# Gate stage: both tiles of a pair turned by VectorE, and the sum of h and the gated embedding made by accumulating transfers

## The chip, the core and the metric

The kernel runs on one core of one Trainium2 chip. The metric is the device time of one execution in microseconds (us). One core has TensorE (in the profile PE for its matmuls, PEld for its weight loads), VectorE (DVE), ScalarE (ACT), GpSimd (POOL) and SyncE (SP); SP, POOL and ACT also issue transfers (DMAs), each in its own queue.

## What is computed

One layer of a streaming encoder on 2048 prompt frames and 32 sample frames of width 1024, in float32:

```python
hn = rmsnorm(h, g_mix)
proj = hn @ w_in                                  # 1024 x 3072
hA, bA, cA, zA, vB, zB = split(proj)              # each 512 wide
yA, new_conv = short_conv_mixer(hA, bA, cA, zA, ...)
yB, new_pool = pooling_mixer(vB, zB, ...)
h = h + concat([yA, yB]) @ w_out
gate = sigmoid(rmsnorm(h, g_ple) @ w_ple_gate)
h = h + (p @ w_ple) * gate
y = rmsnorm(h, g_final)
```

The change touches the last three lines alone: the gate's product of h with `w_ple_gate` (1024 x 1024), the sum `h + e * gate` with the embedding `e = p @ w_ple`, and the closing norm.

## The kernel before

The frames lie in 17 tiles: 16 of 128 frames and one of 32. Three stages follow one another: the input projection with the two mixers, the output projection (which also writes h to device memory as `h_d`, the embedding as `e_d`, and each frame's norm factor to `rs_h`), and the gate stage, in which the change lies. The gate stage takes the 32-frame tile first (`plain`), then seven pairs of 128-frame tiles in a loop, `g0` to `g12` in steps of two, then a last pair with code of its own (`last_pair`, `g14`).

**A pair's products.** A pair is multiplied with the gate weights by a scheme of seven products (Winograd's form of Strassen's multiplication), `seven`, L210. The weights' quarters and their differences (`W["11"]` to `W["T4"]`) stay in SBUF. Every float32 operand is split into a high part (a cast by ACT, L77) and a low part (a subtraction by VectorE, L78), and a product is 12 matmuls of 128x512 (L167): four chunks of the depth, three combinations of high and low part each. The products of a pair run in the order 11, 12, S2, S1, S3, S4, 22, into three banks X, Y and Z. `carry` (ACT copy, L1309) sets aside what a bank holds before it goes on accumulating. `out` ends a quarter of the result: VectorE adds what was set aside (L1317), ACT applies the sigmoid (L1318, or L1315 where nothing was set aside), VectorE multiplies the embedding with it in place (`ee`, L1320) and adds that to h in place (`hh`, L1321). `at` is (tile, half): the outputs come as (0,0), (1,1), (0,1), (1,0).

**A pair's frames.** For the products the tiles of h must stand turned, channels on partitions. `prep_g(i)` gives two steps, called between the products of the pair before (`{2: first, 3: second}`). In `first`, `turned_here(i + 1)` loads the second tile in four transfers of 32 partitions each (L1298), so laid out that one VectorE instruction (`nc.vector.transpose`, which turns every 32x32 block, L1300) leaves it turned in four column groups; `whole` is the view of these groups. In `second`, `turned(i)` loads the first tile in one transfer (L327), ACT copies its halves in another order of channels (`ho`, L1287), and TensorE turns them in eight 128x128 transposes into a PSUM bank (`pth`, L1289). VectorE makes the sums S1 to S4 (L1433), and `put` splits each of the seven operands.

**The end of a tile.** `done_g`, L1325: ACT squares h and sums it (L88), POOL makes the norm factor (L69, L73), VectorE scales h in place by it and the final gain (L1328), and POOL's queue stores it (L1329).

**What sets the order.** The code is written tile by tile, and a planner orders the instructions of each engine by dependences and its own estimates; an engine then takes them strictly in that order, waiting on semaphores. Buffers come from rings: `xh` has 3 buffers for the tiles of h in natural order, `ya` 5 for those of e and for h before and after the turn, `st` 4 for what is set aside and the gate, `cmb` 8 for split operands, PSUM has 6 banks for products and 2 for transposes. A load into a ring waits until the buffer's last reader is done.

Of the kernel before, what the change touches and what calls it, by code (L numbers as in the profile page):

```python
# [12 lines left out]
ALU = mybir.AluOpType  # L13
PSUM = bass.MemoryType.PSUM

P = 128
# [18 lines left out]
def trunk(ctx, tc, x_p, x_s, c_conv, c_pool, p_p, p_s, g_mix, w_in, conv_w, conv_b, pool_w,  # L35
          pool_scale, w_out, g_ple, w_gate, w_ple, g_fin, y_p, y_s, sc_p, sp_p, sc_s, sp_s):
    nc = tc.nc
# [17 lines left out]
    def tbank(name):  # L55
        return ps_t.tile([P, 512], F32, tag="tr", name=name)
# [19 lines left out]
    def split(hi, lo, src, eng=nc.vector):  # L76
        ins = nc.scalar.copy(hi, src)  # L77
        eng.tensor_tensor(lo, src, hi.bitcast(F32), op=ALU.subtract)  # L78
        return ins
# [227 lines left out]
    def ring4(t, name):  # L307
        return t.tile([P, D], F32, tag="t", name=name)
# [15 lines left out]
    def load_rows(pool, name, i, pr, sa=None):  # L324
        r, n = tiles[i]
        t = ring4(pool, f"{name}_{i}")
        nc.sync.dma_start(t[:n], pr[r:r + n] if sa is None else rows_of(pr, sa, r, n))  # L327
        return t

    with ExitStack() as s1:  # L330
# [263 lines left out]
        for c, x in enumerate([*ahead0, short0]):  # L594
            normal(x)
            n = P if c < 3 else DEC
# [511 lines left out]
    with ExitStack() as s2:  # L1108
# [13 lines left out]
        def half_of(x, at, n=P):  # L1122
            return x[at[0]][:n, at[1] * NH:at[1] * NH + NH]
# [96 lines left out]
        for i in range(0, NT - 1, 2):  # L1220
# [6 lines left out]
            if last:  # L1227
                n = tiles[NT - 1][1]
# [50 lines left out]
        def turned(i):  # L1279

            r, n = tiles[i]
            t = load_rows(ya, "hn", i, h_d).rearrange("p (q k c) -> p k q c", q=4, k=KC)
            out = []
            for half in range(2):
                pt = tbank(f"pth_{i}_{half}")
                o = qa.tile([P, KH, P], F32, tag="q", name=f"ho_{i}_{half}")
                nc.scalar.copy(o[:n].rearrange("p k (q c) -> p k q c", q=4), t[:n, half * KH:half * KH + KH])  # L1287
                for k in range(KH):
                    nc.tensor.transpose(pt[:, k * P:k * P + n], o[:n, k], ident[:n, :n])  # L1289
                out.append(pt.rearrange("p (k t) -> p k t", k=KH))  # L1290
            return out

        def turned_here(i):

            r, n = tiles[i]
            t = ring4(ya, f"hn_{i}")
            for q in range(4):
                nc.sync.dma_start(t[q * 32:q * 32 + 32].rearrange("p (g c) -> p g c", g=4),  # L1298
                                  h_d[r:r + P, q * 256:q * 256 + 256].rearrange("(g p) c -> p g c", p=32))
            nc.vector.transpose(t, t)  # L1300
            u = t.rearrange("p (g k t) -> p k g t", g=4, k=KC)
            return u[:, :KH], u[:, KH:]

        def gate_ops(h, e, n, name, i):
            scale = lambda at: rs_h[:n, i + at[0]:i + at[0] + 1]

            def carry(ps, at):
                t = st.tile([P, NH], F32, tag="t", name=f"c_{name}_{at[0]}{at[1]}")
                nc.scalar.copy(t[:n], ps[:n])  # L1309
                return t  # L1310

            def out(ps, c, at):
                if c is None:
                    c = st.tile([P, NH], F32, tag="t", name=f"g_{name}_{at[0]}{at[1]}")
                    nc.scalar.activation(c[:n], ps[:n], AF.Sigmoid, scale=scale(at))  # L1315
                else:
                    nc.vector.tensor_tensor(c[:n], ps[:n], c[:n], op=ALU.add)  # L1317
                    nc.scalar.activation(c[:n], c[:n], AF.Sigmoid, scale=scale(at))  # L1318
                ee, hh = half_of(e, at, n), half_of(h, at, n)
                nc.vector.tensor_tensor(ee, ee, c[:n], op=ALU.mult)  # L1320
                nc.vector.tensor_tensor(hh, hh, ee, op=ALU.add)  # L1321

            return carry, out

# [97 lines left out]
        def prep_g(i):  # L1422

            A = {}
            whole = lambda t: t.rearrange("p k (g t) -> p k g t", g=4)

            def put(q, src, view=lambda t: t):
                A[q] = cmb.tile([P, KH, 2, P], F32R, tag="c", name=f"g{i}_{q}")
                split(view(A[q][:, :, 0]), view(A[q][:, :, 1]), src)

            def comb(q, x, y, op, view=lambda t: t):
                t = ss.tile([P, KH, P], F32, tag="s", name=f"g{i}_f{q}")
                nc.vector.tensor_tensor(view(t), x, y, op=op)  # L1433
                return t

            lower = []

            def first():
                lower.extend(turned_here(i + 1))

            def second():
                a21, a22 = lower
                s1 = comb("S1", a21, a22, ALU.add, whole)
                a11, a12 = turned(i)
                put("11", a11)
                s2 = comb("S2", s1, a11, ALU.subtract)
                s3 = comb("S3", whole(a11), a21, ALU.subtract, whole)
                put("12", a12)
                put("S2", s2)
                s4 = comb("S4", a12, s2, ALU.subtract)  # L1450
                put("S1", s1)
                put("S3", s3)
                put("S4", s4)
                put("22", a22, whole)

            S[i] = A
            return {2: first, 3: second}

        S = {}
        n = tiles[NT - 1][1]  # L1460
        A = short("gl", turned(NT - 1), n)
        for step in prep_g(0).values():
            step()
# [5 lines left out]
        for i in range(0, NT - 3, 2):  # L1469
            A = S.pop(i)  # L1470
            h = [load_rows(xh, "h", i + b, h_d) for b in range(2)]
            e = [load_rows(ya, "e", i + b, e_d) for b in range(2)]
            seven(f"g{i}", A, W, *gate_ops(h, e, P, f"g{i}", i), prep_g(i + 2))
            for b in range(2):
                done_g(i + b, h[b])
# [30 lines left out]
```

## Time and profile before

| | |
|---|---|
| median of 3 runs | 947.03 us (945.0 to 947.33) |
| the profiled execution, its span | 947.7 us |
| instructions in it | 13126 |
| mean granted TensorE clock | 0.989 of full speed |
| gate stage, first product of the first pair to the end | 777.6 to 947.7 us of the span |

The span runs from the first to the last instruction of the profiled execution, which is one execution by itself and not one of the three runs; no time outside its span is recorded. The profile lists for each instruction its engine, its line in the kernel, the tiles it writes and reads, its start and duration, and what ended the idle time before it. The stage tables give busy time by engine in a stretch, with the number of instructions in brackets, then the granted TensorE clock (PEclk), the share of the DMA engines that was busy, and GB/s. Rows of transfers give the size and the median time from issue to landing.

### The profile page before, as it was taken

The page shows a single profiled execution, that of the slowest core. Times are in us where ns is not written, and L with a number is a line of the kernel's source. Part 1 is how long each engine was busy: PE and PEld are TensorE (multiplying, and loading weights), DVE is VectorE, ACT ScalarE, POOL GpSimd, SP SyncE. Part 2 cuts the span into 40 slices and gives each one's busy share as a digit, 9 for nine tenths or more (in the row PEclk, how much of TensorE's full clock was granted, in tenths as well). Part 3 has the DMA queues.
Part 4 walks back from the last instruction along what each step waited for, and adds up shares of the span by engine and source line. Part 5 has one row for each costly group of instructions (what it writes and reads, how often), then busy time and mean ns, then how long its engine had stood idle before and what let it go on. Part 6 is the DMA issues. An engine that isn't in the chain of part 4 may idle for free.

```text
span 947.7 us, 13126 instructions
## 1 busy us (share of the span) xinstructions
PE 925.3 (98%) x4599; PEld 835.1 (88%) x4599; DVE 716.6 (76%) x1212; ACT 480.9 (51%) x890; POOL 136.3 (14%) x262
## 2 busy tenths in 40 slices
PE   6999999898999999999999999999999999999996
PEld 5999999898999999999999987888877868888885
DVE  6697999798677876776777588766554798888995
ACT  5554555463444454443454355434424875556564
POOL 2112323230100110000000011111111000211113
PEclk8999999899999999999999999999999999999999
DMA  8346586676973554628655349874785883566552
GB/s 243 102 127 193 170 273 201 224 219 192 406 273 93 166 183 135 219 56 285 178 175 175 130 146 291 288 200 146 228 253 161 304 285 123 197 232 226 208 206 111
DMA packets 132639, 190.05 MB, mean 201 GB/s; under 512 B 11740, under 2 KB 101084, under 8 KB 131293
## 3 DMA queue, kind: packets, MB, share of 16 engines
q1 hardware_dynamic: 115149, 134.06, 45.1%
q0 software_dynamic: 14688, 49.65, 15.9%
q10 hardware_dynamic: 2736, 5.51, 1.7%
q8 instruction: 36, 0.59, 0.2%
q14 instruction: 30, 0.25, 0.1%
HBM read 129.59 MB, written 59.58 MB: 200 GB/s over the span
## 4 chain that ended last, share of the span: by engine, by line
PE 74%; DMA 5%; DVE 2%; issue 2%; ACT 1%; POOL 1%; POOLq 0%; DVEq 0%; ACTq 0%; SPq 0%
PE x_g L167 9%; PE x_o L167 8%; PE x_zab L571 6%; PE z_g L167 5%; PE x_zbv L571 4%; PE e L102 4%; PE x_ch L571 4%; PE z_o L167 4%; PE z_zab L571 3%; PE z_ch L571 2%; PE y_g L167 2%; PE z_zbv L571 2%; PE y_o L167 2%; PE b L571 2%; PE zb L571 2%; PE h L571 2%
## 5 line engine op out<-in xcount | busy, mean ns | idle before, releaser
L77 ACT CAST y_S<-y_fS 128x512 fp32r<-128x512 f32 x32 | 19.5, 621 | 43.0 <-PE x_o L167 20.2
L571 PE MATMUL x_zab<-B,w_zab_S 128*128 128x416 f32 x168 | 36.6, 367 | 3.1 <-ACT V L866 2.8
L102 PE MATMUL e<-wq,pps 128*128 128x512 f32 (+1 forms) x156 | 38.9, 399 | 0.2 <-ACT pps L77 0.2
L406 DVE SCALAR_TENSOR_TENSOR xt<-xt,rstd_x,g_bc 128x1024 f32<-128x1024 f32 (+2 forms) x18 | 23.1, 1282 | 20.1 <-POOL rstd_x L73 18.7
L571 PE MATMUL z_ch<-B,w_ch_S 128*128 128x416 f32 x168 | 35.3, 360 | 2.4 <-ACT U L866 2.4
L571 PEld LDWEIGHTS x_zab<-B,w_zab_S 128*128 128x128 f32 x168 | 32.7, 197 | 4.4 <-ACT V L866 3.2
L167 PE MATMUL x_g<-wg_b,g_S 128*128 128x512 f32 x128 | 35.9, 390 | 0.0
L167 PE MATMUL x_o<-wo_b,y_S 128*128 128x512 f32 x128 | 35.8, 391 | 0.0
L571 PEld LDWEIGHTS z_ch<-B,w_ch_S 128*128 128x128 f32 x168 | 32.0, 192 | 3.2 <-ACT U L866 2.8
L571 PE MATMUL z_zab<-B,w_zab_S 128*128 128x416 f32 x168 | 34.7, 356 | 0.0
L571 PE MATMUL z_zbv<-B,w_zbv_S 128*128 128x416 f32 x168 | 34.2, 352 | 0.0
L571 PE MATMUL x_zbv<-B,w_zbv_S 128*128 128x416 f32 x168 | 34.1, 351 | 0.0
L571 PE MATMUL x_ch<-B,w_ch_S 128*128 128x416 f32 x168 | 34.0, 351 | 0.0
L102 PEld LDWEIGHTS e<-wq,pps 128*128 128x128 f32 (+1 forms) x156 | 27.4, 182 | 6.9 <-ACT pps L77 0.5
L571 PEld LDWEIGHTS z_zab<-B,w_zab_S 128*128 128x128 f32 x168 | 32.2, 192 | 0.4
L69 POOL TENSOR_SCALAR ms_f<-ssq_f 128x1 f32<-128x1 f32 (+1 forms) x15 | 8.8, 588 | 160.7 <-ACT junk L88 160.7
L571 PEld LDWEIGHTS x_ch<-B,w_ch_S 128*128 128x128 f32 x168 | 31.4, 188 | 0.3
L571 PEld LDWEIGHTS x_zbv<-B,w_zbv_S 128*128 128x128 f32 x168 | 31.3, 188 | 0.3
L571 PEld LDWEIGHTS z_zbv<-B,w_zbv_S 128*128 128x128 f32 x168 | 31.3, 188 | 0.4
L77 ACT CAST y<-y 128x512 fp32r<-128x512 f32 x24 | 14.8, 618 | 30.8 <-PE x_o L167 14.0
L1328 DVE SCALAR_TENSOR_TENSOR h<-h,rstd_f,g_bc 128x1024 f32<-128x1024 f32 (+1 forms) x15 | 19.3, 1284 | 12.7 <-POOL rstd_f L73 12.7
L167 PEld LDWEIGHTS x_o<-wo_b,y_S 128*128 128x128 f32 x128 | 23.9, 188 | 5.1 <-ACT c_o L1132 0.3
(582 smaller groups left out, 2670.3 us busy)
## 6 DMA issues: line engine op xcount, KB each, us to landing
y<-y_d SPq DMA_DIRECT2D x16, 512.0 KB, 6.4
x<-in_x_prompt_dram SPq DMA_DIRECT2D x16, 512.0 KB, 6.5
h_d<-x SPq DMA_DIRECT2D x16, 512.0 KB, 3.4
h<-h_d SPq DMA_DIRECT2D x16, 512.0 KB, 4.6
xt<-in_x_prompt_dram SPq DMA_DIRECT2D x15, 512.0 KB, 12.3
e<-e_d SPq DMA_DIRECT2D x15, 512.0 KB, 5.9
out_dram<-h POOLq DMA_DIRECT2D x14, 512.0 KB, 3.0
p_dT<-T POOLq DMA_DIRECT2D x12, 512.0 KB, 5.0
```

Source lines behind the costliest of these rows:

```text
L69: nc.gpsimd.tensor_scalar(ms[:n], ssq[:n], scalar1=1.0 / D, scalar2=EPS, op0=ALU.mult, op1=ALU.add)
L77: ins = nc.scalar.copy(hi, src)
L102: nc.tensor.matmul(ps[:n], pps[:, a, k, :n], wp[k][b][:, cs], start=k + q == 0, stop=k == 1 and q == 2)
L167: nc.tensor.matmul(ps[:n], lhs[:, k, a, :n], w[b][:, k], start=start and k + q == 0, stop=k == KH - 1 and q == 2, skip_group_check=True)
L406: nc.vector.scalar_tensor_tensor(xt[:n], xt[:n], r[:n], g_bc[:n], op0=ALU.mult, op1=ALU.mult)
L571: nc.tensor.matmul(ps[:, :NB], lhs[:, k, x], b[:, k, y], start=start and k + q == 0, stop=stop and k == KH - 1 and q == 2, skip_group_chec ...
L1328: nc.vector.scalar_tensor_tensor(h[:n], h[:n], rf[:n], g_bc[:n], op0=ALU.mult, op1=ALU.mult)
```

## The change

Two edits, both in the gate stage.

In `gate_ops`, for full tiles, the addition of the gated embedding `ee` to `hh` by VectorE becomes a transfer from `ee` to `hh` (SBUF to SBUF, 128 x 512, 256 KB) that adds to what it finds there; it is issued by POOL. There are four a pair, for the seven pairs of the loop. The 32-frame tile and the last pair keep VectorE's addition.

In `prep_g`, both tiles of a pair are loaded and turned by `turned_here`, in the step `first`. `turned` is used for the 32-frame tile alone. The operands made from the first tile are read from SBUF in the view `whole`, where they were read from PSUM.

```diff
                 ee, hh = half_of(e, at, n), half_of(h, at, n)
                 nc.vector.tensor_tensor(ee, ee, c[:n], op=ALU.mult)
-                nc.vector.tensor_tensor(hh, hh, ee, op=ALU.add)
+                if n == P:
+                    nc.gpsimd.dma_start(hh, ee, accum_op=ALU.add)
+                else:
+                    nc.vector.tensor_tensor(hh, hh, ee, op=ALU.add)
...
-            lower = []
+            both = []

             def first():
-                lower.extend(turned_here(i + 1))
+                both.extend((*turned_here(i + 1), *turned_here(i)))

             def second():
-                a21, a22 = lower
+                a21, a22, a11, a12 = both
                 s1 = comb("S1", a21, a22, ALU.add, whole)
-                a11, a12 = turned(i)
-                put("11", a11)
-                s2 = comb("S2", s1, a11, ALU.subtract)
-                s3 = comb("S3", whole(a11), a21, ALU.subtract, whole)
-                put("12", a12)
+                put("11", a11, whole)
+                s2 = comb("S2", whole(s1), a11, ALU.subtract, whole)
+                s3 = comb("S3", a11, a21, ALU.subtract, whole)
+                put("12", a12, whole)
                 put("S2", s2)
-                s4 = comb("S4", a12, s2, ALU.subtract)
+                s4 = comb("S4", a12, whole(s2), ALU.subtract, whole)
                 put("S1", s1)
                 put("S3", s3)
                 put("S4", s4)
```

## The prediction

> **What bounds the kernel now.** I read the page first, then the stretches of the gate stage, then its timeline engine by engine.
>
> ```profile
> span 947.7 us, 13126 instructions
> ...
> PE 925.3 (98%) x4599; PEld 835.1 (88%) x4599; DVE 716.6 (76%) x1212; ACT 480.9 (51%) x890; POOL 136.3 (14%) x262
> ```
>
> ```profile
> core 0: us, PE busy (x) PEld busy (x) DVE busy (x) ACT busy (x) POOL busy (x), PEclk, DMA share, GB/s
> ...
> 857.40:877.40 20.00, 20.00 (x94) 16.63 (x93) 17.43 (x26) 11.39 (x20) 3.37 (x6) 1.00 0.60 209
> 877.40:897.30 19.90, 19.90 (x94) 16.57 (x92) 17.84 (x27) 11.41 (x20) 3.37 (x6) 1.00 0.60 211
> ```
>
> Each stretch is one pair of the gate stage: PE is busy for all of it at full clock, DVE for 17.4 to 17.8 us of 20. So TensorE is the bound, with VectorE close behind, and nothing waits. The timeline of PE shows what a pair is made of:
>
> ```profile
> 868.54 2.88 PE L167 MATMUL x_g<-wg_b,g_S 128*128 128x512 f32 x12
> 871.26 0.62 PE L167 MATMUL z_g<-wg_d,g_S 128*128 128x512 f32 x2
> 871.72 1.03 PE L1289 MATMUL pth<-ident,ho 128*128 128x128 f32 x8
> 872.51 2.53 PE L167 MATMUL z_g<-wg_d,g_S 128*128 128x512 f32 x10
> 874.87 2.88 PE L167 MATMUL x_g<-wg_T,g 128*128 128x512 f32 x12
> 877.59 2.66 PE L167 MATMUL x_g<-wg_c,g 128*128 128x512 f32 x11
> ```
>
> A product of 12 matmuls takes 2.72 us from start to start (874.87 to 877.59). Seven are 19.04 us. The pair lasts some 19.95 us, so the eight transposes of L1289 hold PE for 0.9.
>
> **The change part by part.** *PE.* The transposes of eight pairs go: 8 x 0.9 = 7.2 us less work on the bound. If nothing new waits, that is the whole effect.
>
> *VectorE.* Per pair it gains one 32x32 turn and loses four additions (`h<-h,e`), and it reads SBUF where it read PSUM. ACT loses two copies `ho<-hn`.
>
> ```profile
> 870.05 1.24 DVE L1300 STREAM_TRANSPOSE hn<-hn 128x1024 f32<-128x1024 f32 x1
> 871.32 0.69 DVE L1433 TENSOR_TENSOR g_fS<-hn 128x512 f32<-128x512 f32 x1
> ...
> 873.40 0.69 DVE L1320 TENSOR_TENSOR e<-e,c_g 128x512 f32<-128x512 f32 x1 [0.79 <-ACT c_g L1318]
> 874.01 0.68 DVE L78 TENSOR_TENSOR g<-pth,g 128x512 fp32r<-128x512 f32 x1
> 874.61 0.68 DVE L1433 TENSOR_TENSOR g_fS<-g_fS,pth 128x512 f32<-128x512 f32 x1
> ```
>
> A 128x512 operation takes 0.68 from either memory and starts 0.60 after the one before it, so VectorE's load falls by 4 x 0.60 - 1.24 = 1.2 us a pair. By load alone, then, VectorE does not become the bound.
>
> *The order, which decides.* Each engine takes its instructions in the order the planner wrote them. In the built program of the change, ACT's order at the end of pair 0 is: the sigmoid of the last product, the square of h of tile 0, the square of h of tile 1, and only then the casts of the next pair's frames, g2_11 first. The square of tile 1 reads the sum h, which now arrives by a transfer, and that transfer's source is made from pair 0's last product. The next pair's first matmul waits for the cast of g2_11. Before, this could not happen: the casts of the next pair (ACT, L77) stood ahead of the squares:
>
> ```profile
> 857.86 0.69 ACT L1315 ACTIVATE g_g<-x_g,rs_h 128x512 f32<-128x512 f32 x1 [0.65 <-PE x_g L167]
> 859.15 0.62 ACT L77 CAST g_S<-g_fS 128x512 fp32r<-128x512 f32 x1 [0.60 <-DVE g_fS L1433]
> 859.67 0.61 ACT L77 CAST g<-hn 128x512 fp32r<-128x512 f32 x1
> ...
> 863.40 1.06 ACT L88 ACTIVATE junk<-h 128x1024 bf16<-128x1024 f32 x1 [1.85 <-issue]
> 864.37 0.19 ACT L88 ACTIVATION_READ_ACCUMULATOR junk<-h 128x1 f32 x1
> ```
>
> ```profile
> 872.65 0.72 ACT L1318 ACTIVATE c_g<-c_g,rs_h 128x512 f32<-128x512 f32 x1 [2.29 <-DVE c_g L1317]
> ```
>
> Going through the built order, I find three kinds of pair. T is the time of one accumulating transfer (256 KB, SBUF to SBUF, from POOL's queue), from issue to landing.
>
> *0 to 2.* From the last product's end: sigmoid 0.69, multiplication 0.68, T, square 1.06 + 0.19, cast 0.62, five handovers between engines at 0.04 (the sigmoid of 872.65 ends at 873.37, its reader on VectorE begins at 873.40), and 0.16 by which the last matmul ends after PE could begin the next (874.87 + 2.88 against 877.59): PE idles 3.6 + T.
>
> *4 to 6, 8 to 10, 12 to 14.* ACT's order is: sigmoid, square of tile 0 of the pair, then the casts. VectorE's order has the scales of the pair before last ahead of the turns, and the final multiplication ahead of the second turn. The chain is longer and goes through POOL, which holds its queue in order. Further rows:
>
> ```profile
> 864.65 0.19 POOL L69 TENSOR_SCALAR ms_f<-ssq_f 128x1 f32<-128x1 f32 x1 [14.79 <-ACT junk L88]
> 864.92 0.56 POOL L73 TENSOR_TENSOR rstd_f<-ms_f,nhalf 128x1 f32<-128x1 f32 x1
> ...
> 867.44 0.61 POOL L1329 DMA_DIRECT2D out_dram<-h  x1
> ```
>
> ```profile
> 865.51 1.29 DVE L1328 SCALAR_TENSOR_TENSOR h<-h,rstd_f,g_bc 128x1024 f32<-128x1024 f32 x1 [0.99 <-POOL rstd_f L73]
> ```
>
> ```profile
> h<-h_d SPq DMA_DIRECT2D x16, 512.0 KB, 4.6
> ...
> out_dram<-h POOLq DMA_DIRECT2D x14, 512.0 KB, 3.0
> ...
> gs<-in_w_ple_gate_dram POOLq DMA_DIRECT2D x16, 256.0 KB, 8.6
> ...
> kept_zbv<-s_zbv POOLq DMA_DIRECT2D x3, 256.0 KB, 2.7
> ...
> kept_zab<-s_zab POOLq DMA_DIRECT2D x3, 256.0 KB, 3.8
> ```
>
> ```profile
> SPq L327 <- DMA out_dram<-h: 54.1, 13, 6.9
> ```
>
> The last row says why POOL is in it: h has three buffers, so the load of a pair's second h waits until the earlier pair's first h has been stored. Say pair 4 begins at 0. VectorE ends the multiplication of e_2 (pair 2's) at about 5.1, being its ninth instruction about there (9 x 0.60, the first begun 0.3 before). Then: transfer T; square 1.25; statistic 0.9; scale 1.29; store of h_2 3.0; load of h_5 4.6; POOL issues the sum of h_5 that waited for it, 0.65, and behind it the sum of h_4, T; square of h_4 1.25; cast 0.62; ten handovers 0.4. The pair lasts 19.1 + 2T, against 19.95. On SP's queue, the last loads of hn for tile 6 stand behind that load of h_5; they land some 3 us after it is issued, before the turn needs them.
>
> *2 to 4, 6 to 8, 10 to 12.* Here the casts stand ahead of the squares, so frames are ready in time. But a scale (1.29) stands ahead of the first low part on VectorE, so the product just begun stops for 1.1 (pair 2) or 1.6 us (6 and 10) at its third matmul; less the 0.9 of the transposes.
>
> *T.* No accumulating transfer is in the trace. Below: the quiet row of the same size and queue from SBUF, 2.7 (kept_zbv). It reads only one side, and the sum reads two. Above: 8.6 for a 256 KB load by the same queue. I take 3.8, the kept_zab row: same size, queue and source, nearest to a transfer that has some traffic beside it. For the range I allow 2.4 to 6. The Trainium skill, "DMA: Bandwidth & Descriptors", section "Anatomy of one DMA", states 2.0 us plus bytes over 436 GB/s for a transfer by this path: 2.6 us here, an estimate from that page. The quiet row agrees with it; the page does not price the second read. By 2.6 the sum would give some 970.
>
> *The clock.* PE has not idled that long in this stage. What a thin stretch does to it shows at the kernel's start:
>
> ```profile
> 12.00:14.00 2.00, 0.68 (x6) 0.41 (x5) 1.75 (x2) 2.00 (x5) 0.74 (x3) 1.00 1.08 259
> 14.00:16.00 2.00, 0.69 (x7) 0.46 (x6) 2.00 (x4) 1.85 (x4) 0.21 (x1) 0.98 0.38 100
> 16.00:18.00 2.00, 1.98 (x11) 1.85 (x12) 2.00 (x4) 1.12 (x4) 0.00 (x0) 0.50 0.61 178
> 18.00:20.00 2.00, 2.00 (x8) 1.90 (x7) 2.00 (x6) 2.00 (x5) 0.00 (x0) 0.50 1.01 401
> 20.00:22.00 2.00, 2.00 (x7) 1.92 (x6) 2.00 (x4) 0.53 (x2) 0.00 (x0) 0.50 0.89 327
> 22.00:24.00 2.00, 2.00 (x10) 1.89 (x10) 0.50 (x2) 0.00 (x0) 0.00 (x0) 0.81 0.70 209
> ```
>
> After 4 us in which PE was busy for a third, the granted clock was 0.50 for nearly 7 us, in which 3.4 us were lost. Four gaps of 6 to 7.5 us would cost 4 x 3.4 = 13.6 at most. Part of it falls into the stop at the third matmul, and the gap may itself use up the slow time. I take 1.5 a gap, 6 us in all, with 0 and 13.6 as ends. The Trainium skill, "TensorE: Matmul & The Clock Gate", part 1, speaks against this change: after one idle window of about 3.4 us the array runs at half clock until a busy window has passed, so each gap would cost at least 1.7 us, 6.8 in all, an estimate. The trace agrees on the 0.50; its slow time was two such windows.
>
> *Sum, with T = 3.8, against the span.* First pair: the tile that came in one load now comes in four.
>
> ```profile
> 774.14 2.46 SPq L1298 DMA_DIRECT2D hn<-h_d  x4
> ```
>
> Three issues more are 1.8 us by this row, and a turn on VectorE takes the place of transposes on PE; I take 1.6 (0 to 2.5). 0 to 2: 19.04 + 3.6 + 3.8 - 19.95 = +6.5. Three times 19.1 + 7.6 - 19.95 = +6.75, so +20.2 (for the last I count the product that ran early before, 2.7, with the pair). Pair 2: 1.1 - 0.9 = +0.2; pairs 6 and 10: 0.7 each, +1.4. In the last pair the same low parts come late, +1.2. Together 1.6 + 6.5 + 20.2 + 0.2 + 1.4 + 1.2 = +31.1, and 6 for the clock: +37. The span of 947.7 lies 0.7 above the runs' median of 947.03, so I count from 947: **984 us**.
>
> **The rivals.** *Cheap transfers.* T of 2.4 and no clock loss. The sum moves by 7T (one T in the first gap, two in each of three), so it is 31.1 - 9.8 = +21: 968 us. For it: SBUF has no far memory to wait for. It cannot fall much further: with T at nothing, the last product's sigmoid, multiplication, turn (1.24) and cast still stand in a row before the next pair, 3.5 us of idle PE at four places, less the transposes: about +16, 963 us. *Dear transfers.* T of 6, with the clock as above: 31.1 + 15.4 + 6 = +52.5, 999 us. For it: two reads to one write, beside loads of h and e; the 8.6 row. *Faster.* The transfers and turns hide behind the matmuls and the 7.2 us go: 940 us. This needs the cast of the next first frame to be done 0.16 us after the last product, so neither a square nor a turn may stand between. It decides at four places; the built order has them there, so only if the chip runs another order. *Not as it says.* That no sum goes by POOL is excluded by the built order, four a pair.
>
> **How the numbers follow.** Forecast 0.54 (970 to 994), cheap 0.20, dear 0.22, faster 0.03, and 0.01 for something that cancels out near no change. The range takes both rivals: 966 to 1003. Faster by over 0.3% (about what a measurement of this kernel tells from no change) 0.03, within 0.01, slower 0.96.
>
> **What would show it.** Right: PE idle of 6 to 8 us before `x_g<-wg_c,g` at four places, pairs 0 to 2, 4 to 6, 8 to 10 and 12 to 14, released by ACT's cast L77; ahead of it ACT idle before L88, ended by a DMA `h<-e`; pairs alternating at about 27 and 21 us; PEclk under 1.00 behind the gaps. Wrong: pairs of 19 us throughout; a landing of `h<-e` far from 3.8, which moves the time by seven times the difference; or gaps that hang on loads of hn and not on squares.

## The result and the profile after

| | before | after |
|---|---|---|
| median of 4 runs each | 946.26 us (945.0 to 947.33) | 1006.9 us (1004.25 to 1008.5) |
| ratio, 95% interval | | 1.0644 (1.0625 to 1.0664) |
| span of the profiled execution | 947.7 us | 1006.3 us |
| PE busy | 925.3 us | 931.3 us |

Slower by 60 us; the forecast was 984, in a range of 966 to 1003. The busy times in the profile of the changed kernel:

```profile
PE 931.3 (93%) x4535; PEld 832.7 (83%) x4535; DVE 710.6 (71%) x1192; ACT 473.6 (47%) x874; POOL 155.9 (15%) x290
```

The 64 transposes are gone, and PE is busy for 6 us more; its idle time grew from 22.4 (947.7 - 925.3) to 75.0 us. Where, its timeline shows (start, duration, engine, line, names, shapes, number; in brackets the idle time before and what ended it):

```profile
778.70 0.73 PE L167 MATMUL x_g<-wg_c,g 128*128 128x512 f32 x2 [2.25 <-ACT g L77]
...
805.04 1.22 PE L167 MATMUL x_g<-wg_c,g 128*128 128x512 f32 x2 [6.95 <-ACT g L77]
...
827.75 2.88 PE L167 MATMUL x_g<-wg_c,g 128*128 128x512 f32 x12
840.13 3.02 PE L167 MATMUL x_g<-wg_b,g_S 128*128 128x512 f32 x12 [1.34 <-ACT c_g L1309]
846.76 3.06 PE L167 MATMUL x_g<-wg_T,g 128*128 128x512 f32 x12 [0.90 <-DVE c_g L1317]
860.77 1.22 PE L167 MATMUL x_g<-wg_c,g 128*128 128x512 f32 x2 [10.96 <-ACT g L77]
...
883.15 2.88 PE L167 MATMUL x_g<-wg_c,g 128*128 128x512 f32 x12
...
916.88 1.22 PE L167 MATMUL x_g<-wg_c,g 128*128 128x512 f32 x2 [11.39 <-ACT g L77]
...
940.19 2.88 PE L167 MATMUL x_g<-wg_c,g 128*128 128x512 f32 x12
...
965.15 0.46 PE L1372 MATMUL ptp_l<-ident,p_l 128*128 128x128 f32 x2 [2.35 <-DMA p_l<-in_p_prompt_dram]
973.42 1.22 PE L167 MATMUL x_g<-wg_c,g 128*128 128x512 f32 x2 [7.81 <-ACT g L77]
```

Each `x_g<-wg_c,g` begins a pair. The pairs last 26.3, 22.7, 33.0, 22.4, 33.7, 23.3 and 33.2 us, where they lasted 19.95. PE stands still at four places, 37.1 us in all, released by ACT's cast; at the last of them (12 to 14) it had already waited 2.35 us for a load of the last pair, `p_l`, so that the four stops come to 39.5. Inside the long pairs come two stops that the forecast did not have: the product S2 (`wg_b`) waits for an ACT copy, and the last product (`wg_T`) for VectorE.

The group of squares says what ACT waited for (busy time, mean ns of one, then idle time before and its releaser):

```profile
L88 ACT ACTIVATE junk<-h 128x1024 bf16<-128x1024 f32 (+1 forms) x15 | 15.8, 1056 | 43.1 <-DMA h<-e 40.2
```

The timelines of POOL, SP and ACT at the boundary 4 to 6 show one such wait whole:

```profile
850.26 2.64 POOL L1322 DMA_DIRECT2D h<-e  x3 [4.36 <-DMA h<-h_d]
...
851.23 0.34 SPq L327 DMA_DIRECT2D h<-h_d  x1
851.61 7.76 SPq L327 DMA_DIRECT2D e<-e_d  x2
...
859.07 1.06 ACT L88 ACTIVATE junk<-h 128x1024 bf16<-128x1024 f32 x1 [8.52 <-DMA h<-e]
...
860.12 1.12 ACT L77 CAST g<-hn 128x512 fp32r<-128x512 f32 x2
```

POOL issues three sums in a row, SP loads of 512 KB of h and e beside them. The square starts 8.8 us after the first issue, and PE, behind square and cast, 1.7 us after that. In mid-pair another square holds ACT's copy (`c_g<-x_g`, for which PE stops at 840.13). On VectorE a scale then waits for the factor made from the next square, and behind that scale and a turn (844.90) stands the addition for which PE stops at 846.76:

```profile
838.45 1.06 ACT L88 ACTIVATE junk<-h 128x1024 bf16<-128x1024 f32 x1 [3.55 <-DMA h<-e]
...
839.51 0.57 ACT L1309 COPY c_g<-x_g 128x512 f32<-128x512 f32 x1
...
843.69 1.29 DVE L1331 SCALAR_TENSOR_TENSOR h<-h,rstd_f,g_bc 128x1024 f32<-128x1024 f32 x1 [1.85 <-POOL rstd_f L73]
```

And the clock, in stretches of 2 us (PEclk stands before the DMA share and GB/s):

```profile
810.00:812.00 2.00, 2.00 (x6) 1.53 (x6) 1.34 (x2) 0.74 (x2) 0.35 (x1) 0.54 0.71 207
...
852.00:854.00 2.00, 0.00 (x0) 0.00 (x0) 1.97 (x3) 0.00 (x0) 0.90 (x2) 0.70 1.05 152
854.00:856.00 2.00, 0.00 (x0) 0.00 (x0) 0.42 (x1) 0.00 (x0) 0.00 (x0) 0.50 1.11 315
...
864.00:866.00 2.00, 2.00 (x6) 1.52 (x6) 2.00 (x5) 0.00 (x0) 1.20 (x2) 0.50 0.66 256
866.00:868.00 2.00, 2.00 (x10) 1.61 (x9) 2.00 (x4) 1.73 (x3) 0.43 (x1) 0.89 0.41 90
```

At the boundary 4 to 6 PE stopped at 849.8 (860.77 - 10.96). A mean of 0.70 in the stretch from 852 puts the fall to 0.50 at about 852.8; 0.89 in the stretch from 866 puts the return at about 866.4, 5.7 us after PE went on. At the boundary 0 to 2 the 0.54 puts the return at about 811.8, 6.8 us after the restart at 805.04. Read in the same way from stretches of 1 us, the fall came 3.5 us after the stop at 0 to 2 and 5.3 us after it at 8 to 10, and the return 7.6 us after the restart at 8 to 10 and 5.7 us after it at 12 to 14.

### The profile page after: what moved, and what is told of

Its sections match the earlier page's. It is cut to its first block, busy times and chain, and to the rows that moved or that the text cites. A ratio compares the mean times of both kernels' runs of the same rounds, so it can differ in the third digit from the quotient of the medians.

```text
span 1006.3 us, 13093 instructions
## 1 busy us (share of the span) xinstructions
PE 931.3 (93%) x4535; PEld 832.7 (83%) x4535; DVE 710.6 (71%) x1192; ACT 473.6 (47%) x874; POOL 155.9 (15%) x290
## 5 line engine op out<-in xcount | busy, mean ns | idle before, releaser
L167 PE MATMUL x_g<-wg_c,g 128*128 128x512 f32 x96 | 34.2, 511 | 41.1 <-ACT g L77 39.4
L167 PEld LDWEIGHTS x_g<-wg_c,g 128*128 128x128 f32 x96 | 23.1, 252 | 50.5 <-ACT g L77 41.4
L1318 ACT ACTIVATE c_g<-c_g,rs_h 128x512 f32<-128x512 f32 x21 | 15.2, 723 | 47.8 <-DVE c_g L1317 47.8
L1322 POOL DMA_DIRECT2D h<-e x28 | 24.2, 953 | 80.0 <-DVE e L1320 63.1
L88 ACT ACTIVATE junk<-h 128x1024 bf16<-128x1024 f32 (+1 forms) x15 | 15.8, 1056 | 43.1 <-DMA h<-e 40.2
L167 PEld LDWEIGHTS x_g<-wg_b,g_S 128*128 128x128 f32 x128 | 23.8, 188 | 11.0 <-ACT c_g L1309 6.1
```

What stands on the lines that cost most here:

```text
L88: ins = nc.scalar.activation(junk[:n], x[:n], AF.Square, accum_out=ssq[:n])
L167: nc.tensor.matmul(ps[:n], lhs[:, k, a, :n], w[b][:, k], start=start and k + q == 0, stop=k == KH - 1 and q == 2, skip_group_check=True)
L1322: nc.gpsimd.dma_start(hh, ee, accum_op=ALU.add)
```

## The experiments

Ratios are to the kernel before on the same chip, with 95% intervals. First the two edits, each by itself.

**e1_turns.** In the changed kernel, the additions back on VectorE:

```diff
-                if n == P:
-                    nc.gpsimd.dma_start(hh, ee, accum_op=ALU.add)
-                else:
-                    nc.vector.tensor_tensor(hh, hh, ee, op=ALU.add)
+                nc.vector.tensor_tensor(hh, hh, ee, op=ALU.add)
```

> The turning edit alone: VectorE turns both tiles of a pair, the sums of h and the gated embedding stay additions on VectorE. Theory A (the turning edit holds both hn buffers until the operands are made, so the next pair's hn come late and ACT's squares of h get ahead of the casts; each such boundary stops PE by sigmoid, multiplication, addition, square and cast, some 4 to 5 us): +20 to +30, so 966 to 977 us, with gaps of 4 to 6 us before x_g<-wg_c,g at four places. Theory B (all the loss is the transfers): 940 to 948 us, no such gaps.

978.05 us, 1.0330 (1.0303 to 1.0356): some 32 of the 60 us come from the turns, with no transfer in play. The time lies just above theory A's; theory B falls. PE, ACT and VectorE at the same boundary:

```profile
847.33 5.73 PE L167 MATMUL x_g<-wg_c,g 128*128 128x512 f32 x12 [5.13 <-ACT g L77]
...
845.62 1.06 ACT L88 ACTIVATE junk<-h 128x1024 bf16<-128x1024 f32 x1 [0.27 <-DVE h L1321]
...
846.67 1.12 ACT L77 CAST g<-hn 128x512 fp32r<-128x512 f32 x2
...
844.75 0.69 DVE L1321 TENSOR_TENSOR h<-h,e 128x512 f32<-128x512 f32 x1
845.37 1.24 DVE L1300 STREAM_TRANSPOSE hn<-hn 128x1024 f32<-128x1024 f32 x1
```

Two chains end together at 846.6 to 846.7: the squares on ACT, and on VectorE the last addition and the turn behind it. At 0 to 2 the stop is 6.84 us long, also without any transfer; there the turn (800.30) stands behind a scale (799.10).

**e2_sums.** In the kernel before, only the sums by transfers (the second edit of the change alone).

> The sums alone: accumulating transfers for the sum, the first tile of a pair still turned by TensorE, as in the kernel before. Its built order has the casts ahead of the squares. Theory A (a sum costs when a square in front of the next casts waits for it, and not otherwise): 947 to 960 us; what is left are stops in the middle of a pair where ACT's copies of the products stand behind a square. Theory B (the transfers themselves are what costs, whatever the order): 985 us or more.

970.2 us, 1.0253 (1.0228 to 1.0277), between the two theories. The parts, 32 and 24, make 56 of the 60. No pair begins late here; PE stops ahead of S2 instead, for 0.8 to 3.75 us in six pairs, behind an ACT copy held by a square. One of them, on PE and on ACT:

```profile
832.75 4.61 PE L167 MATMUL x_g<-wg_b,g_S 128*128 128x512 f32 x12 [2.92 <-ACT c_g L1309]
...
831.08 1.06 ACT L88 ACTIVATE junk<-h 128x1024 bf16<-128x1024 f32 x1 [4.94 <-DMA h<-e]
```

**e3_plain.** `accum_op=ALU.add` left away in the changed kernel, so that h itself is missing from the sum.

> The changed kernel with a plain copy of the gated half onto the half of h in place of the accumulating one: h itself is left out of the sum, nothing else differs. If accumulating is what makes a transfer slow (two reads, or a slower mode), landing falls from a median of 4.6 to 2.4 to 3, three queued ones no longer need 8 us, and the time is 970 to 985 us. If it is the queue, POOL's issue or the traffic beside it, landing and time stay: 1000 to 1008 us.

994.37 us, 1.0504 (1.0469 to 1.0540); landing, median, 3.8 us against 4.6. Adding accounts for some 12 us; a plain transfer waits as well. Both ranges missed.

**e4_casts_first.** In the changed kernel, the closing work of a pair behind the next pair's last cast:

```diff
-                put("22", a22, whole)
+                last_cast.append(put("22", a22, whole))
...
-            for b in range(2):
-                done_g(i + b, h[b])
+            with tc.issue_after(last_cast[-1].ins):
+                for b in range(2):
+                    done_g(i + b, h[b])
```

> The changed kernel with one change of order: the squares of h, scales and stores of a pair are issued after the last cast of the next pair's operands. Theory A: the four gaps of 7 to 11 us before x_g<-wg_c,g go with their clock loss; what remains is the turn and cast behind the last multiplication and hn loads that come late: 958 to 972 us, granted clock back near 1.00. Theory B (transfers slow whatever waits for them: they hold POOL's queue and the h buffers): 985 us or more, with the gaps now ended by loads of h, e or hn.

977.6 us, 1.0332 (1.0306 to 1.0357). That takes 29 us off, between the theories and less than A had: gaps of 2.1 to 3.4 us are left at four places, behind a turn that stands after the last multiplication, and stops of 2.2 to 2.5 before S2 at three.

**e6_turns_casts_first.** The same edit in e1_turns.

> Turns alone (978.1 us), with the squares, scales and stores of a pair issued behind the last cast of the next pair's operands. Theory A (squares ahead of casts are most of the loss): gaps of 5 us before x_g<-wg_c,g shrink to the turn, subtraction-free cast and handovers behind the last addition, 2 to 3 us, and the time to 960 to 970 us. Theory B (late hn loads set the gaps, whatever stands ahead of the casts): 975 us or more.

976.66 us, 1.0318 (1.0299 to 1.0336): no gain over 978.05. Theory A falls, but not for B's reason. With the squares out of the way the cast waits for the turn, and the turn for VectorE's additions:

```profile
848.76 1.14 ACT L77 CAST g<-hn 128x512 fp32r<-128x512 f32 x2 [3.40 <-DVE hn L1300]
```

**p1_transfers.** The price of a transfer by itself: the kernel before with this behind its end, in all combinations of one or three, accumulating or plain, alone or beside two loads.

```diff
+        def sums(n):
+            for i in range(n):
+                nc.gpsimd.dma_start(hh[i][:, :NH], ee[i][:, :NH], accum_op=ALU.add)
...
+        def loads():
+            for i in range(2):
+                nc.sync.dma_start(ll[i], h_d[(8 + i) * P:(9 + i) * P])
```

> The kernel before, with a probe behind its end: transfers of 256 KB (128 x 512 from SBUF to SBUF, POOL's queue) alone on an idle chip, one or three in a row, accumulating or plain, with or without two loads of 512 KB by SP issued beside them; twelve rounds of each kind of three. The kernel's own time is not the point. Theory A (the accumulating transfer is slow in itself and three share the same engines): one accumulating 3.0 to 3.6 us from issue to landing, the last of three 6 to 8 us on a quiet chip, one plain 2.2 to 2.6 and the last of three plain 3 to 4. Theory B (the loads beside them are what stretches them): the last of three accumulating ones lands within 4.5 us when nothing else runs and needs 8 only beside the loads; plain ones behave alike.

Three rounds were run; the rows are from the first, and the others differ from it by at most 0.7 us. Issue and landing of one transfer, in order: accumulating and plain alone, then accumulating and plain beside the loads (the last column is us from issue to landing):

```profile
hh<-ee POOLq DMA_DIRECT2D x1, 256.0 KB, 3.4
...
hh<-ee POOLq DMA_DIRECT2D x1, 256.0 KB, 2.3
...
hh<-ee POOLq DMA_DIRECT2D x1, 256.0 KB, 7.0
...
hh<-ee POOLq DMA_DIRECT2D x1, 256.0 KB, 4.6
```

Three accumulating ones, first alone, then beside the loads: POOL's issues, and VectorE's instructions that wait for each landing.

```profile
978.46 2.64 POOL L1498 DMA_DIRECT2D hh<-ee  x3 [6.34 <-DVE ll L1485]
...
981.91 0.16 DVE L1485 TENSOR_TENSOR tok<-tok,hh 128x1 f32<-128x1 f32 x1 [3.47 <-DMA hh<-ee]
...
984.81 0.16 DVE L1485 TENSOR_TENSOR tok<-tok,hh 128x1 f32<-128x1 f32 x1 [1.21 <-DMA hh<-ee]
...
992.46 2.65 POOL L1498 DMA_DIRECT2D hh<-ee  x3 [4.19 <-DVE ll L1485]
...
1000.49 0.16 DVE L1485 TENSOR_TENSOR tok<-tok,hh 128x1 f32<-128x1 f32 x1 [8.05 <-DMA hh<-ee]
...
1003.00 0.16 DVE L1485 TENSOR_TENSOR tok<-tok,hh 128x1 f32<-128x1 f32 x1 [1.08 <-DMA hh<-ee]
```

Alone the three are there 3.5 and, the last, 6.4 us after the first issue; beside two loads 8.0 and 10.5. Three plain ones are there after 2.4 and 4.0 us alone, after 5.0 and 7.6 beside the loads. Theory A's numbers hold on the quiet chip, but beside loads a single transfer takes twice as long and three land four us later, as theory B had it: both are at work. The 8.8 at the boundary 4 to 6, where the square waits for one of three, lies between 8.0 for the first and 10.5 for the last. The Trainium skill, "DMA: Bandwidth & Descriptors", section "Anatomy of one DMA", gives 2.6 us for this size, an estimate from that page; the plain transfer alone agrees (2.3), the accumulating one took 3.4, and beside loads neither does.

**e9_sums_squares_late.** In e2_sums, the closing work of a pair behind the third ACT copy of the next:

```diff
+                if before:
+                    with tc.issue_after(copies[-1].ins):
+                        for b in range(2):
+                            done_g(before[0] + b, before[1][b])
```

> The sums alone (the kernel before with accumulating transfers, measured at 970.2 us), and the squares of h, scales and stores of a pair issued behind the third copy of the next pair's products on ACT instead of ahead of it. Theory A (the transfers cost because a square that waits for a landing holds ACT's copies, and PE waits for those): the stops before x_g<-wg_b,g_S released by ACT c_g L1309 go, 947 to 956 us. Theory B (the transfers cost by themselves, through POOL's queue, the h and e buffers or contention): 964 us or more.

958.55 us, 1.0136 (1.0112 to 1.0160), again between. The stops ahead of S2 are all gone, and with them half of the sums' loss. In their place PE waits up to 2.0 us for the turned first tile, whose h is loaded late (`ho<-hn` ended by `DMA hn<-h_d`):

```profile
871.50 1.14 ACT L1287 COPY ho<-hn 128x512 f32<-128x512 f32 x2 [1.24 <-DMA hn<-h_d]
```

**e7_turns_own_buffer.** In e1_turns, the first tile's h in two halves in the two buffers that `ho` had:

```diff
+        def turned_halves(i):
+            r, n = tiles[i]
+            u = []
+            for half in range(2):
+                t = qa.tile([P, NH], F32, tag="q", name=f"hh_{i}_{half}")
+                for q in range(4):
+                    at = q * 256 + half * 128
+                    nc.sync.dma_start(t[q * 32:q * 32 + 32].rearrange("p (g c) -> p g c", g=4),
+                                      h_d[r:r + P, at:at + 128].rearrange("(g p) c -> p g c", p=32))
+                nc.vector.transpose(t, t)
+                u.append(t.rearrange("p (g k t) -> p k g t", g=4, k=KH))
+            return u
```

> Turns alone (additions stay on VectorE; with both tiles in the ring of e and hn this measured 978.1 us), but the first tile's h comes in two halves into the two buffers of ho that the change leaves empty, by eight loads of 512-byte rows, and is turned there; so one buffer of the ring less is held. Theory A (the turning edit costs because it holds two buffers of that ring until the operands are made, which pushes casts behind squares): pairs of 19.5 to 21 us from the third on and 950 to 963 us. Theory B (the second turn on VectorE is itself too much for VectorE): 970 us or more, VectorE without idle time.

954.52 us, 1.0092 (1.0069 to 1.0114): theory A. 24 of the 32 us of the turns go; pairs from the third on last 19.1 to 21.0 us. One gap of some length is left:

```profile
799.97 5.39 PE L167 MATMUL x_g<-wg_c,g 128*128 128x512 f32 x12 [5.10 <-ACT g L77]
```

**e10_own_turns_first.** In e7, the turns ahead of the last two multiplications, whose results nobody on PE waits for:

```diff
-                nc.vector.tensor_tensor(ee, ee, c[:n], op=ALU.mult)
+                if n == P and at in ((0, 1), (1, 0)):
+                    with tc.issue_after(turns[-1].ins):
+                        nc.vector.tensor_tensor(ee, ee, c[:n], op=ALU.mult)
+                else:
+                    nc.vector.tensor_tensor(ee, ee, c[:n], op=ALU.mult)
```

> Turns alone with the first tile's h in its own two buffers (954.5 us), and in every pair VectorE's turns for the next pair issued ahead of its last two multiplications (of halves 01 and 10). Theory A (what is left there is the gap of 5.1 us and its clock loss before pair 2, where the turn stands behind the last multiplications and additions though its data have landed): that gap falls to 2 to 3 us without clock loss, 946 to 951 us. Theory B (VectorE is full): 953 us or more.

944.75 us, 0.9971 (0.9953 to 0.9988): 0.3% faster than the kernel before and better than theory A had it: some 2 of the 7.2 us that the transposes took. From the third pair on the pairs last 19.0 to 19.6 us (the third from 812.05 to 831.09), and the stop before pair 2 is down to 1.38:

```profile
792.04 0.73 PE L167 MATMUL x_g<-wg_c,g 128*128 128x512 f32 x2 [1.38 <-ACT g L77]
```

**e12_ring_turns_first.** In e1_turns, the closing work behind the cast of the next pair's operand 12 (the first tile's second half of channels, `put("12", a12)`; not a frame) and the turns ahead of the last multiplication alone, that of half 10.

> Turns alone with both tiles in the ring of e and hn (978.1 us), with both orders mended: squares, scales and stores behind the cast of frame 12 of the next pair, and the next pair's turns ahead of the last multiplication. Theory A (the gap stands on two orders at once, so mending the squares alone gave nothing, 976.7 us): gaps before x_g<-wg_c,g of 5 us fall to 1.5 to 3, time 960 to 968 us. Theory B (the loads of hn land too late in the ring, and the turn waits for them wherever it stands): 972 us or more, with the gaps ended by DMA hn<-h_d ahead of the turn.

972.99 us, 1.0284 (1.0265 to 1.0303), a miss for A: the gaps did fall, to 2.24 us at five of seven places, but now every pair has one, and six of the seven cost clock as well. Two of them:

```profile
849.67 0.73 PE L167 MATMUL x_g<-wg_c,g 128*128 128x512 f32 x2 [2.24 <-ACT g L77]
850.80 4.14 PE L167 MATMUL x_g<-wg_c,g 128*128 128x512 f32 x10
873.09 0.73 PE L167 MATMUL x_g<-wg_c,g 128*128 128x512 f32 x2 [2.24 <-ACT g L77]
874.22 2.55 PE L167 MATMUL x_g<-wg_c,g 128*128 128x512 f32 x10
```

No wait for `hn<-h_d` stands ahead of the turns, so theory B's reason is not seen either. What is left at 873.09 is the turn (871.15), which still stands behind the multiplication and the addition of half 01 (869.81 and 870.54), and the cast behind it:

```profile
872.42 1.14 ACT L77 CAST g<-hn 128x512 fp32r<-128x512 f32 x2 [0.84 <-DVE hn L1302]
```

In e10 the turns stand ahead of both, so this run does not tell what the buffers alone do.

**e5_early_half.** Now the sums. In the changed kernel, only the halves that are ready early by transfers:

```diff
-                if n == P:
+                if n == P and at[0] == at[1]:
```

> The changed kernel (1006.9 us) with only the sums of the early halves (00 and 11) made by transfers, the late ones (01 and 10) by VectorE. Theory A (what the sums add to the turns' loss is the wait of a square for the landing of a late half): nearly all of the sums' part goes, 972 to 982 us, as with the turns alone (978.1). Theory B (the transfers cost by their traffic and POOL's queue, late or early): half of it goes, 988 to 996 us.

978.08 us, 1.0334 (1.0315 to 1.0352), the same as the turns alone (978.05). Two transfers of four cost nothing there; the late two make up all that the sums added.

**e13_own_all_sums** and **e11_own_early_sums.** e10 with all four sums by transfers, and with the early two.

> All of the change (both tiles turned by VectorE, all four sums by accumulating transfers) on the mended base that measured 944.8 us with additions on VectorE: first tile's h in its own two buffers, turns ahead of the last two multiplications. Theory A (a transfer lands 3.4 us after its issue when alone but 7 to 8 beside loads or in a row, and ACT's squares of the late halves hold copies and casts for that long): slower than the same base by 10 to 25 us, 955 to 970 us, with ACT idle before L88 ended by DMA h<-e. Theory B (with the order mended the landings hide): 950 us or less.

> As e10, and the sums of the two halves that are ready early in a pair (00 and 11) made by accumulating transfers, the late two (01 and 10) by VectorE. Theory A (a sum costs nothing where nothing waits for its landing soon, and it frees VectorE of 2 x 0.60 us a pair): 939 to 946 us, faster than the kernel before. Theory B (every transfer costs by traffic and by POOL's queue): slower than e10, 950 us or more.

968.35 us, 1.0233 (1.0212 to 1.0254), theory A; and 949.71 us, 1.0041 (1.0027 to 1.0056), where theory A expected a gain; it is just short of theory B's 950. On the mended order four transfers a pair cost 23.6 us and the early two 5.

**e14_own_pool_adds.** e11 with POOL adding, instead of a transfer: `nc.gpsimd.tensor_tensor(hh, hh, ee, op=ALU.add)`.

> The mended base (944.8 us) with the early halves' additions (00 and 11) done by POOL itself instead of by transfers (949.7 us). Theory A (the transfers lost there by their traffic beside the loads of h and by queue order, not by POOL's place in the program): without the transfers' traffic and with an addition whose end is near, 938 to 946 us. Theory B (what cost was that POOL stands waiting for h in the order of its queue, before statistics and stores): 948 us or more.

947.22 us, 0.9999 (0.9983 to 1.0014): half of the 5 us, between the theories. In the transfers' rows over the seven pairs, loads slow down where sums run beside them. The first tile's h and h itself in e10, e11 and e14:

```profile
h<-h_d SPq DMA_DIRECT2D x14, 512.0 KB, 4.0
...
hh<-h_d SPq DMA_DIRECT2D x56, 64.0 KB, 4.9
```

```profile
h<-h_d SPq DMA_DIRECT2D x14, 512.0 KB, 5.8
...
hh<-h_d SPq DMA_DIRECT2D x56, 64.0 KB, 5.7
h<-e POOLq DMA_DIRECT2D x14, 256.0 KB, 6.4
```

```profile
h<-h_d SPq DMA_DIRECT2D x14, 512.0 KB, 4.2
...
hh<-h_d SPq DMA_DIRECT2D x56, 64.0 KB, 3.8
```

The slowdown of the loads is shown; that it makes just the other half is not.

## Why the prediction was wrong, step by step

Direction, places and releasers were right: four stops at the pairs named, released by ACT's cast, with ACT ahead of L88 waiting for `h<-e`, pairs alternating, PEclk below 1.00 behind. e1 and e2 show that both edits do it: the order that lets squares precede casts comes with the turns, and the sums lengthen what then stands in the row.

The size was 21.5 us low (37.1 forecast, 58.6 by the spans). By terms:

- *0 to 2*, 26.4 forecast, 26.3 measured: here T was near 3.8. The second square began 3.4 us after the last sum's issue (799.90 to 803.33).
- *The three long pairs*, T mis-sized. They last 33.0, 33.7 and 33.2 us where 26.7 were forecast: 19.8 of the 21.5 us. The chain is the one forecast. In the pair from 827.75 on, the multiplication of e_2 ends after 5.1 us, as reckoned. But the first sum took 5.3 us where 3.8 were counted (833.11 to 838.45), the load of h 5.1 where 4.6 were (845.17 to 850.26), and the last step, issue and landing of the sums, 8.8 where 0.65 + 3.8 were (850.26 to 859.07; 9.1 and 8.4 in the other two pairs): 6.4 us together. I had counted two transfers in a row at the end; the trace has three, beside two loads. The row from which I took 3.8, kept_zab, writes to device memory and not to SBUF, and it comes from an earlier stage (95 to 218 us). 8.6, the row quoted above it, was nearer; the range stopped at 6. p1 gives the price in its two situations: 3.4 and 7.0 for one, 8.0 and more for three.
- *Stops inside the long pairs*, left out: 1.34 + 0.90, 1.61 + 0.90 and 1.90 + 0.89 are 7.5 us. I followed the squares to the casts only; ACT's copies of the products also stand behind them, and VectorE's additions behind scales that wait for the squares. By the trace these stops did not lengthen the long pairs: the chain above runs through ACT, POOL, SP and VectorE, and PE would have waited the longer at the end of the pair. That is argued from the chain; no run takes these stops alone away. In e2, where no such chain holds the next pair, the stops ahead of S2 are what PE waits for, and e9, which moves the squares behind the copies, shows them gone.
- *The clock*: 6 taken, with 13.6 as the far end. PE is busy for 6.0 us more without its 7.2 us of transposes, so matmuls took 13.2 longer; by the granted clock in stretches of 1 us, 12.1 of it is the slow clock. It falls into the short pairs and the last one. The short ones last 22.7, 22.4 and 23.3 us where 20.15, 20.65 and 20.65 and 1.5 of clock each were counted: 2.5 of the miss. It would be more, but the stops at the third matmul were 0.33, 0.69 and 0.69 where 1.1, 1.6 and 1.6 were counted. I took it that the stop would use up the slow time. It does not: after stops of 7 and of 11 us the clock stayed at 0.50 for 6.8 and 5.7 us after PE went on. The Trainium skill, "TensorE: Matmul & The Clock Gate", part 1, would have the half clock after an idle window of some 3.4 us. The trace is near it but not at it: the clock fell 3.5, 3.0 and 5.3 us after PE had stopped, and in e12 stops of 2.24 us were enough at some places. The slow time after the restart was longer than one such window.

These are 19.8 + 2.5 us; the first pair took 0.7 off (forecast +1.6, and it came 0.9 later, 777.83 before, 778.70 after), and the last pair came out as counted.

Two side sums of the prediction are off: with T of 2.6 and the 6 us for the clock it gives 976 us and not 970, and with T at nothing its rows give some +15 and not +16.

Of the rivals, "dear transfers" (T of 6, 999 us) was nearest, though its price applies only beside loads; "cheap" is refuted by p1 wherever h and e are being loaded. The 7.2 us of "faster" were out of reach in the order that was built, as the prediction had it; in another order (e10), with additions on VectorE, some 2 of them come.

What e1's theory A held for the root of the turns' loss, that two tiles of the next pair sit in the ring of e and hn, fits e7 and e10: with the first tile in buffers of its own 24 of the 32 us go, and with the turns put forward the rest. But e7 also turns in halves (0.70 each), so the two aren't separated; e12 leaves the ring and puts the turns only partly forward, so it doesn't separate them either; and what the planner reckoned with is in no trace. That part of the cause stays open.

## What to carry over

An engine that takes its queue in order makes every wait in it everybody's: before moving a sum to a transfer, list what stands behind each reader of the sum, casts and copies alike, and price the landing beside the transfers that run at that very place (here 8 to 9 us, not 3.4). Moving work to an engine with room pays only if its place in that engine's queue is early enough: the turns cost 32 us behind the last additions, 8 with the first tile in buffers of its own, and gained 2 when they were also put ahead of those additions. A transfer took load off VectorE, which was not the bound, and the loads beside it grew slower (h from 4.0 to 5.8 us). On the mended order two sums a pair lost 5 us and four lost 24; in the changed kernel the two early ones lost nothing (e5).

## What was not expected of the hardware

An accumulating transfer of 256 KB from SBUF to SBUF took 3.4 us alone and 7.0 beside two loads of 512 KB, a plain one 2.3 and 4.6; in a row, alone, further accumulating ones landed some 1.45 us apart (981.91 to 984.81, two steps). POOL issued an accumulating one in 0.85 us, a plain one in 0.54 (medians in the changed kernel and in e3).

The length of a stop alone did not decide whether the clock fell: in e12 stops of 2.24 us before equal products were followed by 4.14 us at one place (granted clock 0.50 from 852 to 854) and 2.55 at another (1.00 throughout) for the same ten matmuls.
